# Three column pairs taken together at the FFN's start, another tail, and a crossed placement of every second head pair in PSUM

## The chip, the cores and the metric

The kernel runs on one core of a Trainium2 chip. The metric is the device time of one execution in microseconds (us); the time before is the median of three timed runs. One further execution was recorded by the hardware profiler, and every row that is quoted comes from it. Engines go by short names: PE is TensorE's matrix multiply, PEld its weight load, DVE is VectorE, ACT is ScalarE, POOL is GpSimd, SP is the queue that issues most of the DMAs.

## The reference, cut to what matters

One layer of a hybrid decoder is applied to a prompt of 256 tokens and to 8 x 4 decoded tokens. All 288 tokens go through the same weights.

```python
h = _rmsnorm(x, norm_pre_mix)
z = h @ w_in                                            # 2048 -> 8480 columns
ya, new_wkv = _rwkv7_branch(zs_mix, st_wkv, ...)        # 16 heads of 64, a state [64, 64] each
yb, new_pool = _pool_branch(zp, st_pool, ...)
m = sigmoid(zga) * (ya @ w_branch_a) + sigmoid(zgb) * (yb @ w_branch_b)
x = x + _rmsnorm(m @ w_out, norm_post_mix)
gate, up = split(_rmsnorm(x, norm_pre_ffn) @ w_ffn_in)  # 2048 -> 2 x 5632
f = (gelu(conv(gate)) * up) @ w_ffn_out
x = x + _rmsnorm(f, norm_post_ffn)

def step(s, inp):                                       # the scan of the RWKV-7 branch, per token
    r_t, w_t, k_t, v_t, a_t, b_t = inp
    sa = einsum('bhvk,bhk->bhv', s, a_t)
    s = s * w_t[:, :, None, :] + sa[..., None] * b_t[:, :, None, :] + v_t[..., None] * k_t[:, :, None, :]
    return s, einsum('bhvk,bhk->bhv', s, r_t)
```

## The kernel before, in words

**Dense work.** Channels lie on the 128 partitions, the 288 tokens (`N`) on the free axis. A weight column block of 128 outputs is a list of *units*, each 4 k-tiles of 128x128. A unit is loaded by SP (`load_to`, L176, `raw`), split into two fp32r parts `whi` (ACT, L199) and `wlo` (DVE, L200) by `split_to`, and used by `three` (L259): `whi`·`xh`, `whi`·`xl`, `wlo`·`xh`, three matmuls of 288 columns per k-tile. `take(u)` (L264) splits three units ahead and loads nine ahead. `dense` makes one output column in one PSUM bank; `dense_together` (L288) makes several columns side by side, unit by unit, so that each x part that arrives late is used for all columns.

**PSUM.** There are eight banks: pool `psa` has three (tag `acc`), `psb` three (tag `s`), `psg` two (tag `g`).

**RWKV.** The 16 heads are worked on in four groups `g` of four heads: `i` in 0, 1 is the channel tile (a pair of heads), `par` in 0, 1 the head of the pair, which lies on partitions 0-63 or 64-127 (`HALF`). For each group `front` prepares decay, keys and receptances (`AR`, `KB`), `late` forms the products `ps_g` (L637), a triangular inverse on DVE (L699 to L702; a trip through DRAM, `dA` and `dW`), then the four-chunk `chain` (`ps_x`, `ps_u`, `ps_s`, `ps_y`) and, beside it, `sample` for the decoded tokens (`ps_sg`, `ps_sl`, `ps_st`), and `finish` normalizes and transposes the outputs (`ps_yt`). These generators are stepped by three lanes from inside the dense work: `lane2`, with `late`, makes two steps for each unit, and `yield n` waits n steps. So these small matmuls stand between dense ones in PE's queue. The lanes fix the order in which the program is written down; a scheduler then orders each engine's queue by its own estimate, and an instruction under `pin` stays behind what was written before it on its engine. All queues run in order.

**Where small matmuls sit.** A matmul with 64 rows of weights and 64 outputs uses one quarter of the array: its input half gives the rows, the PSUM half that it writes gives the columns. Before, head `par` reads half `par` and writes half `par` (`ps_sg`, `ps_st`, `ps_y`, `ps_yt`) for both `i`, or reads one half and writes all 128 outputs (`ps_g`).

**The turn.** After the 16 columns of `w_out` (L1165), `rstd_of` (L348) sums the squares over partitions with a matrix of ones, takes a root on ACT and a reciprocal on DVE; `second_parts(k)` (L1185) makes the residual `x2[k]` and its parts `xh`, `xl`; `second_squares` sums their squares for the next norm. `dense_together` then takes the first four `w_ffn_in` columns (two pairs of gate and up).

**The tail** (L1286 to L1311): `rstd_spread` (L359) makes the last scale with tiny matmuls and spreads it into PSUM; DVE multiplies it into the four quarters `fq`, and the residual is added on PE (with the identity), on POOL or on DVE before SP stores the tile.

Of the kernel before, what the change touches and what calls it, by code (L numbers as in the profile page):

```python
# [18 lines left out]
P = 128  # L19
# [22 lines left out]
FA = 2  # L42
BT = 5
IWAIT = 3
IWORK = 300
# [61 lines left out]
def hybrid_step(ctx: ExitStack, tc: tile.TileContext, t):  # L107
# [56 lines left out]
    for f0, nf in THIRDS:  # L164
        ins = []
        if f0 == 0:
            u = add_together([wf[0], wf[NF], wf[1], wf[NF + 1]])
            ins = [(u[0], u[1]), (u[2], u[3])]
# [5 lines left out]
    cursor = {"load": 0, "split": 0}  # L174

# [13 lines left out]
    def split_to(u):  # L189
        while cursor["split"] <= min(u, len(units) - 1):  # L190
# [5 lines left out]
            hi = wp.tile([P, UK, P], F32R, tag="whi", name="whi", bufs=4)  # L196
            lo = wp.tile([P, UK, P], F32R, tag="wlo", name="wlo", bufs=4)
# [66 lines left out]
    def take(u):  # L264
        split_to(u + 3)
        load_to(u + 9)
# [65 lines left out]
    last = [None]  # L332

    def scaled_parts(k, src, scale, where=xp):
        h, l = (where.tile([P, N], F32R, tag=f"x{p}{k}", name=f"x{p}{k}") for p in "hl")
        act.activation(out=h, in_=src, func=AF.Copy, scale=scale)
# [166 lines left out]
    heads = [(i, par) for i in range(G) for par in range(2)]  # L503
    ready, past, k2 = {}, set(), []

    def front(g, rr, kx, vv, lora):
# [21 lines left out]
        ps = psb.tile([P, NC2 + G, 2], F32, tag="s", name="ps_n")  # L528
        for i, par in heads:
            h, o = HALF[par], HALF[1 - par]  # L530
            for c in range(NCH):
                pe.matmul(ps[o, c * G + i], sq[h, i, c * C:(c + 1) * C], ones[h, 0:2], start=True, stop=True)
        for i, par in heads:
            h = HALF[par]
            pe.matmul(ps[UR[par], NC2 + i], sq[h, i, TP:], ones[h, 0:2], start=True, stop=True,
                      tile_position=(h.start, UR[par].start))
# [4 lines left out]
        for par in range(2):  # L541
            dve.tensor_scalar(wr[UR[par], NC2:], ps[UR[par], NC2:, 0:1], 1e-24, None, op0=ALU.max)
            dve.reciprocal(wr[UR[par], NC2:], wr[UR[par], NC2:])
# [78 lines left out]
    def late(g):  # L622
        yield lambda: g in ready
        yield 4
# [6 lines left out]
        for c2 in range(0, NCH, 2):  # L631
            pss = [psg.tile([P, 2 * G, 2 * C], F32, tag="g", name="ps_g") for _ in range(2)]
            for dc in range(2):
                c = c2 + dc
                for i, par in heads:
                    h = HALF[par]
                    pin(pe.matmul(  # L637
                        pss[par][:, dc * G + i, :],
                        KB[h, c, i, :, :].rearrange("p s t -> p (s t)"),
                        AR[h, :, i, c * C:(c + 1) * C],  # L640
                        start=True, stop=True,
                    ))
# [35 lines left out]
        psv = psb.tile([P, G, C], F32, tag="s", name="ps_sv")  # L678
        for i, par in heads:
            h = HALF[par]  # L680
            pe.matmul(psv[VR[par], i], vv[h, i, TP:], ident[h, h], start=True, stop=True, tile_position=(h.start, VR[par].start))
        for par in range(2):
            act.copy(out=UV0[VR[par]], in_=psv[VR[par]])
# [6 lines left out]
        def inverse():  # L690
# [6 lines left out]
            for tt in range(1, 32):  # L697
# [6 lines left out]
                if work > IWORK:  # L704
                    work = 0
                    yield
# [26 lines left out]
        def sample():  # L733
# [14 lines left out]
            ps = psb.tile([P, 3, G, C], F32, tag="s", name="ps_sg")  # L748
            for i, par in heads:
                h = HALF[par]  # L750
                pin(pe.matmul(ps[h, 0, i], KBs[h, i].rearrange("p s t -> p (s t)"), AR[h, :, i, TP:], start=True, stop=True))
            for i, par in heads:
                h = HALF[par]
                pin(pe.matmul(ps[h, 1, i], KBd[h, i].rearrange("p s t -> p (s t)"), ident[h, h], start=True, stop=True))
            for i in range(G):
                for b in range(NB):
                    for par in range(2):
# [673 lines left out]
```

## Time and profile before

| | us |
|---|---|
| median of three timed runs | 1668.98 (1668.06 to 1670.8) |
| the profiled execution, its own time | 1666.09 |
| its span, first to last instruction | 1664.3 |
| PE busy | 1627.8 |
| DVE busy | 1104.5 |
| ACT busy | 814.6 |
| POOL busy | 382.0 |

PE's busy time counts from the start of a matmul to its end, and neighbours overlap: a dense matmul is shown as 0.30 us long, but the next one starts 0.13 us after it. So the distance from start to start is what tells what a piece of PE's work costs. A row of the timeline gives start, duration, engine, line, operation, tiles and count, and in brackets the idle time of the engine before it with the instruction that ended it. An fp32 matmul (not fp32r) is two records. PEclk is the clock that TensorE was granted, 1.00 at full speed.

### The profile page before, as it was taken

How to read it: one execution, taken by the hardware profiler on the slowest of the kernel's cores; microseconds unless marked ns; L12 is line 12 of the kernel's file. 1: busy time of each engine (PE TensorE's matmuls, PEld its weight loads, DVE VectorE, ACT ScalarE, POOL GpSimd, SP SyncE). 2: the span in 40 equal slices, each digit the busy share in tenths (PEclk: the TensorE clock that was granted, in tenths of full speed). 3: DMA queues.
4: the chain of work that ended last, by engine and by line, in shares of the span. 5: the costliest groups of instructions: out<-in, count | busy, mean ns of one | idle time of the engine just before them, and what ended most of it. 6: DMA issues, size and time to landing. Idle time of an engine off the chain costs nothing.

```text
span 1664.3 us, 35679 instructions
## 1 busy us (share of the span) xinstructions
PE 1627.8 (98%) x13398; PEld 1589.1 (95%) x13398; DVE 1104.5 (66%) x2192; ACT 814.6 (49%) x1492; POOL 382.0 (23%) x629
## 2 busy tenths in 40 slices
PE   7999999999999999999899999999999999999998
PEld 6989989989989999999799999999999999999997
DVE  6799778778777857644876665446666555666654
ACT  5544445445445435545565554445545433455554
POOL 4593452343242022400321110001111000111112
PEclk9999999999999999999899999999999999999999
DMA  7435445435535548744254445554444555444553
GB/s 245 159 114 185 157 160 178 158 122 187 188 109 184 189 145 275 236 165 165 96 178 166 166 165 168 167 166 165 167 168 166 166 166 168 165 167 165 176 167 105
DMA packets 157229, 278.95 MB, mean 168 GB/s; under 512 B 25584, under 2 KB 32240, under 8 KB 157056
## 3 DMA queue, kind: packets, MB, share of 16 engines
q1 hardware_dynamic: 151104, 259.16, 48.6%
q0 software_dynamic: 5664, 16.77, 2.8%
q8 instruction: 105, 1.72, 0.4%
q10 hardware_dynamic: 288, 0.74, 0.1%
q14 instruction: 68, 0.56, 0.1%
HBM read 262.67 MB, written 13.93 MB: 166 GB/s over the span
## 4 chain that ended last, share of the span: by engine, by line
PE 88%; DVE 5%; POOL 2%; DMA 2%; issue 1%; ACT 0%; SPq 0%; DVEq 0%; POOLq 0%
PE acc L262 27%; PE acc L260 27%; PE acc L261 27%; DVE wlo L200 1%; DVE wt L699 1%; DMA dW<-wt 1%; PE ps_g L637 1%; DVE wt L702 0%; PE ps_sg L759 0%; POOL win L998 0%; PE ps_s L877 0%; DMA W<-dW 0%; PE ps_st L807 0%; PE ps_y L892 0%; PE ps_u L867 0%
## 5 line engine op out<-in xcount | busy, mean ns | idle before, releaser
L200 DVE TENSOR_TENSOR wlo<-raw,whi 128x512 fp32r<-128x512 f32 x928 | 655.3, 709 | 416.3 <-ACT whi L199 407.6
L199 ACT CAST whi<-raw 128x512 fp32r<-128x512 f32 x928 | 572.7, 619 | 696.5 <-PE acc L261 650.3
L260 PE MATMUL acc<-xh,whi 128*128 128x288 f32 x2736 | 814.8, 299 | 14.1 <-ACT whi L199 9.0
L262 PE MATMUL acc<-xh,wlo 128*128 128x288 f32 x2736 | 812.1, 297 | 5.2 <-DVE wlo L200 5.2
L261 PE MATMUL acc<-xl,whi 128*128 128x288 f32 x2736 | 812.3, 297 | 0.0
L260 PEld LDWEIGHTS acc<-xh,whi 128*128 128x128 f32 x2736 | 517.3, 189 | 18.7 <-ACT whi L199 9.6
L262 PEld LDWEIGHTS acc<-xh,wlo 128*128 128x128 f32 x2736 | 520.2, 190 | 9.9 <-DVE wlo L200 6.1
L261 PEld LDWEIGHTS acc<-xl,whi 128*128 128x128 f32 x2736 | 521.3, 191 | 1.5 <-issue 0.3
L262 PE MATMUL acc<-ah,wlo 128*128 128x288 f32 x704 | 208.7, 296 | 0.0
L260 PE MATMUL acc<-ah,whi 128*128 128x288 f32 x704 | 208.0, 296 | 0.0
L261 PE MATMUL acc<-al,whi 128*128 128x288 f32 x704 | 205.2, 292 | 0.0
L1223 POOL COPY cout<-gt 128x2 f32<-128x2 f32 x44 | 30.8, 700 | 591.7 <-DVE gt L1219 591.7
L261 PEld LDWEIGHTS acc<-al,whi 128*128 128x128 f32 x704 | 134.2, 191 | 0.0
L260 PEld LDWEIGHTS acc<-ah,whi 128*128 128x128 f32 x704 | 132.2, 188 | 0.0
L262 PEld LDWEIGHTS acc<-ah,wlo 128*128 128x128 f32 x704 | 131.9, 187 | 0.0
L1231 POOL TENSOR_TENSOR cv<-cv,rstd_ffn 128x288 f32<-128x288 f32 x44 | 36.8, 837 | 73.9 <-ACT cv L1230 73.1
L699 DVE TENSOR_TENSOR wt<-wt,Ab 128x16 f32<-128x16 f32 (+30 forms) x124 | 52.6, 425 | 1.3
L442 POOL TENSOR_TENSOR df<-zt 128x256 f32<-128x256 f32 (+1 forms) x27 | 23.1, 855 | 100.3 <-DVE zt L440 80.0
L1227 DVE SCALAR_TENSOR_TENSOR cv<-gt,vec,cv 128x255 f32<-128x255 f32 x88 | 43.0, 489 | 0.0
L1188 POOL TENSOR_TENSOR x<-x,og 128x288 f32<-128x288 f32 x11 | 12.9, 1171 | 114.8 <-DVE og L1187 114.8
L262 PE MATMUL acc<-ybh,wlo 128*128 128x288 f32 x128 | 38.2, 298 | 0.7 <-DVE wlo L200 0.7
L260 PE MATMUL acc<-ybh,whi 128*128 128x288 f32 x128 | 38.8, 303 | 0.0
(309 smaller groups left out, 1589.1 us busy)
## 6 DMA issues: line engine op xcount, KB each, us to landing
raw<-in_w_ffn_in SPq DMA_DIRECT2D x352, 256.0 KB, 3.0
raw<-in_w_in SPq DMA_DIRECT2D x264, 256.0 KB, 3.4
raw<-in_w_ffn_out SPq DMA_DIRECT2D x176, 256.0 KB, 2.7
raw<-in_w_out SPq DMA_DIRECT2D x64, 256.0 KB, 3.0
raw<-in_w_branch_b SPq DMA_DIRECT2D x32, 256.0 KB, 3.0
raw<-in_w_branch_a SPq DMA_DIRECT2D x32, 256.0 KB, 4.0
xr<-in_xT SPq DMA_DIRECT2D x8, 288.0 KB, 5.6
tga<-th POOLq DMA_DIRECT2D x16, 144.0 KB, 3.6
```

Of the source, the lines that this page charges most:

```text
L199: act.copy(out=hi[:, a:b, :m], in_=w[:, a:b, :m])
L200: dve.tensor_tensor(lo[:, a:b, :m], w[:, a:b, :m], hi[:, a:b, :m].bitcast(F32), op=ALU.subtract)
L260: pe.matmul(ps, hi, xh, start=start, stop=False)
L261: pe.matmul(ps, hi, xl, start=False, stop=False)
L262: pe.matmul(ps, lo, xh, start=False, stop=stop)
L442: pool.tensor_tensor(df[:m, :TP], zt[:m, 0:TP], zt[:m, 1:ZB], op=ALU.subtract)
L637: pin(pe.matmul(pss[par][:, dc * G + i, :], KB[h, c, i, :, :].rearrange("p s t -> p (s t)"), AR[h, :, i, c * C:(c + 1) * C], start=True, s ...
L699: dve.tensor_tensor(tmp[:, :, :n], Wb[:, :, :n], Ab[:, :n, tt].unsqueeze(1).to_broadcast([P, 8, n]), op=ALU.mult)
L1188: (dve if k < 2 or k % 4 == 0 else pool).tensor_tensor(x2[k], x2[k], og[k], op=ALU.add)
L1223: pool.tensor_copy(cout[:, f, 0:2], gt[:, TP - 2:TP])
L1227: dve.scalar_tensor_tensor(cv[:, s:TP], gt[:, 0:TP - s], w, cv[:, s:TP], op0=ALU.mult, op1=ALU.add)
L1231: pool.tensor_tensor(cv, cv, rst3, op=ALU.mult)
```

## The change

It has these parts.

1. At the turn three pairs, six columns (`TOG`), are made together in place of four. `dense_by_k` goes k-tile by k-tile through all six columns in the first unit, two k-tiles at a time after it. For that, `look` makes `take` split six units ahead from column 14 of `w_out` on, and odd units take their parts from a further SBUF pool `wp2`.
2. `rst2` comes from `rstd_spread`; `second_parts` is queued so that `x2[0]` comes directly after the first product; the squares for the next norm are queued behind all parts.
3. The tail multiplies all four quarters first; then nine tiles get their residual on PE, three on DVE, four on POOL; stores are of one or two tiles.
4. `side(i, par)` puts the second pair (`i` = 1) on the other PSUM half: `ps_n` (decoded part), `ps_sv`, `ps_sg`, `ps_st`, `ps_y`, `ps_yt`. The two pairs then write two banks, one from `psb` and one from `psg`, or two from `psg`. `ps_g` is cut into 64x64 pieces in the order (half 0, half 0), (1, 1), (0, 1), (1, 0). `ps_w` and `ps_n` move from `psb` to `psg`. In `ps_y` the product with `UV` comes ahead of the one with the state.
5. Pace: the inverse yields by `IWORK` 370 with its remainder kept (300 before, remainder dropped); `late(0)` starts after 9 steps, not 4, and waits 11, not 16, ahead of the transposes; two more groups of matmuls (`ps_w12`, `ps_x` with `UV`) are pinned.

```diff
+TOG = 3
-IWORK = 300
+IWORK = 370
...
+            where = late_pool[0] if late_pool and i % 2 else wp
+            hi = where.tile([P, UK, P], F32R, tag="whi", name="whi", bufs=4)
...
     def take(u):
-        split_to(u + 3)
-        load_to(u + 9)
+        split_to(u + look[0])
+        load_to(u + look[0] + 6)
...
+    def dense_by_k(uss, xh, xl, pools):
+        pss = [p.tile([P, 512], F32, tag=tag, name="acc") for p, tag in pools]
+        for c in range(len(uss[0])):
+            w = []
+            step = 2 if c else 1
+            for j0 in range(0, 4, step):
+                for i, (ps, us) in enumerate(zip(pss, uss)):
+                    if j0 == 0:
+                        w.append(take(us[c]))
+                    for j in range(j0, j0 + step):
+                        k = 4 * c + j
+                        three(ps[:, :N], w[i][0][:, j], w[i][1][:, j], xh[k], xl[k], k == 0, k == KD - 1)
+                    if j0 + step == 4:
+                        advance()
+        return pss
...
+    def side(i, par):
+        return par ^ (i % 2)
...
-                ps = psb.tile([P, 512], F32, tag="s", name="ps_w")
+                ps = psg.tile([P, 512], F32, tag="g", name="ps_w")
...
-        yield 4
+        yield 4 if g else 9
...
-                for i, par in heads:
-                    h = HALF[par]
-                    pin(pe.matmul(
-                        pss[par][:, dc * G + i, :],
-                        KB[h, c, i, :, :].rearrange("p s t -> p (s t)"),
-                        AR[h, :, i, c * C:(c + 1) * C],
-                        start=True, stop=True,
-                    ))
+                for i in range(G):
+                    for par, slot in ((0, 0), (1, 1), (0, 1), (1, 0)):
+                        h = HALF[par]
+                        pin(pe.matmul(
+                            pss[par][HALF[slot], dc * G + i, :], KB[h, c, i, slot, :], AR[h, :, i, c * C:(c + 1) * C],
+                            start=True, stop=True,
+                        ))
...
-                if work > IWORK:
-                    work = 0
-                    yield
+                if work >= IWORK:
+                    yield work // IWORK
+                    work %= IWORK
...
-            ps = psb.tile([P, 3, G, C], F32, tag="s", name="ps_sg")
+            pst = [psg.tile([P, 3, C], F32, tag="g", name="ps_sg") for _ in range(G)]
...
+            for b in range(NB):
+                for i, par in heads:
+                    h, q = HALF[par], HALF[side(i, par)]
+                    pin(pe.matmul(pst[i][q, 2], arm[h, i, b * C:(b + 1) * C], S0[h, i, b, :], start=b == 0, stop=b == NB - 1))
...
+            for i, par in heads:
+                h, q = HALF[par], HALF[side(i, par)]
+                pin(pe.matmul(psts[i][h], BKs[q, i], uxs[i][q], start=True, stop=True))
...
-        yield 2 * WWAIT + (0 if g else 16)
+        yield 2 * WWAIT + (0 if g else 11)
...
+                psy = [p.tile([P, 512], F32, tag=tag, name="ps_y") for p, tag in ((psb, "s"), (psg, "g"))]
+                for i, par in heads:
+                    pe.matmul(
+                        psy[i][HALF[side(i, par)], 0:C], Gm[:, par, c * G + i, 0:C], UV[:, c * G + i, par, :],
+                        start=True, stop=c == 0,
+                    )
                 if c:
                     for i, par in heads:
                         h = HALF[par]
+                        pe.matmul(
+                            psy[i][HALF[side(i, par)], 0:C], AR[h, 0, i, c * C:(c + 1) * C], S[h, i, :],
+                            start=False, stop=True,
+                        )
...
                 for par in range(2):
-                    h, r = HALF[par], slice(64 * par, 64 * par + 32)
-                    pe.matmul(ps[h, TP:N], Yt[r, NC2 + i, :], ident[r, r], start=True, stop=True, tile_position=(h.start, h.start))
+                    h, q = HALF[par], HALF[side(i, par)]
+                    pe.matmul(ps[h, TP:N], Yt[q, NC2 + i, :], ident[q, q.start:q.start + 32], start=True, stop=True)
...
+        if j == 14:
+            look[0] = 2 * TOG
+            late_pool.append(wp2)
...
-    rst2 = rstd_of([acc2, sq], "post", ep)
+    rst2 = rstd_spread([acc2, sq], ep)
...
-        with tc.issue_after(paced[k - AHEAD]) if k >= AHEAD else ExitStack():
+        with tc.issue_after(paced[k - AHEAD] if k >= AHEAD else ends[0]) if k else ExitStack():
             dve.tensor_tensor(og[k], og[k], rst2, op=ALU.mult)
...
+        with tc.issue_after(last[0].ins), tc.issue_after(last_hi[0].ins):
+            for k in range(KD):
+                second_squares(k)
...
-                    pss = dense_together(uss, xh, xl, [(psa, "acc")] * 2 + [(psg, "g")] * 2)
+                    pss = dense_by_k(uss, xh, xl, [(psa, "acc")] * 3 + [(psg, "g")] * 2 + [(psb, "s")])
...
+    on_pe = {0: psg, 1: psg, 2: psa, 4: psa, 5: psa, 8: psb, 9: psg, 14: psg, 15: psa}
+    on_dve = (11, 12, 13)
...
     for q in range(4):
         pin(dve.tensor_tensor(fq[q], fq[q], rst4.unsqueeze(1).to_broadcast([P, 4, N]), op=ALU.mult))
+    for j in range(16):
+        if j in on_pe:
...
+            pin(pe.matmul(sums[j][:, :N], ident, f_sb[j], start=False, stop=True))
+            pin(act.copy(out=f_sb[j], in_=sums[j][:, :N]))
+        else:
+            pin((dve if j in on_dve else pool).tensor_tensor(f_sb[j], f_sb[j], x2[j], op=ALU.add))
...
+        if j in (1, 5, 9, 15):
+            store(j - 1, 2)
+        elif j not in (0, 4, 8, 14):
+            store(j)
```

More of the change, by code (lines that the diff above doesn't have):

```diff
@@ L174, in hybrid_step @@
     cursor = {"load": 0, "split": 0}
+    late_pool, look = [], [3]
     def load_to(u):
@@ L526, in front @@
                 act.activation(out=dst[:, i], in_=ps[:, :N], func=AF.Tanh, scale=0.5, bias=der[:, row, m:m + 1])
-        ps = psb.tile([P, NC2 + G, 2], F32, tag="s", name="ps_n")
+        ps = psg.tile([P, NC2 + 1, 2], F32, tag="g", name="ps_n")
         for i, par in heads:
@@ L532, in front @@
                 pe.matmul(ps[o, c * G + i], sq[h, i, c * C:(c + 1) * C], ones[h, 0:2], start=True, stop=True)
+        psn = [psg.tile([P, 2], F32, tag="g", name="ps_ns"), ps[:, NC2]]
         for i, par in heads:
             h = HALF[par]
-            pe.matmul(ps[UR[par], NC2 + i], sq[h, i, TP:], ones[h, 0:2], start=True, stop=True,
-                      tile_position=(h.start, UR[par].start))
+            pe.matmul(psn[i][HALF[side(i, par)]], sq[h, i, TP - 32:], ones[h, 0:2], start=True, stop=True)
         wr = kp.tile([P, NC2 + G, 1], F32, tag="wr", name="wr", bufs=2)
@@ L677, in late @@
             act.copy(out=UV[HALF[par], :, par, :], in_=ps[HALF[par]].rearrange("p (a v) -> p a v", v=C))
-        psv = psb.tile([P, G, C], F32, tag="s", name="ps_sv")
+        psv = [p.tile([P, C], F32, tag=tag, name="ps_sv") for p, tag in ((psb, "s"), (psg, "g"))]
         for i, par in heads:
[L680 to L683, printed above, removed]
+            h, r = HALF[par], VR[side(i, par)]
+            pe.matmul(psv[i][r], vv[h, i, TP:], ident[h, h], start=True, stop=True, tile_position=(h.start, r.start))
+        for i in range(G):
+            for r in VR:
+                act.copy(out=UV0[r, i], in_=psv[i][r])
         yield 3
@@ L772, in sample @@
             for i in range(G):
-                act.activation(out=BKs[:, i], in_=ps[:, 1, i], func=AF.Copy, scale=wr[:, NC2 + i])
+                act.activation(out=BKs[:, i], in_=pst[i][:, 1], func=AF.Copy, scale=wr[:, NC2 + i])
             for i in range(G):
@@ L803, in sample @@
             for i in range(G):
-                pst = psb.tile([P, NB, C], F32, tag="s", name="ps_st")
-                for par in range(2):
-                    h = HALF[par]
-                    pin(pe.matmul(pst[h], BKs[h, i], uxs[i][h], start=True, stop=True))
-                psts.append(pst)
+                psts.append(psb.tile([P, NB, C], F32, tag="s", name="ps_st"))
+            for i, par in heads:
+                h, q = HALF[par], HALF[side(i, par)]
+                pin(pe.matmul(psts[i][h], BKs[q, i], uxs[i][q], start=True, stop=True))
             for i in range(G):
@@ L1284, in hybrid_step @@
     pool.dma_start(out=t["o_conv"], in_=cout)
-    banks = [(psg, "g"), (psg, "g"), (psa, "acc"), (psa, "acc"), (psb, "s"), (psa, "acc"), (psg, "g"), (psg, "g")]
+    on_pe = {0: psg, 1: psg, 2: psa, 4: psa, 5: psa, 8: psb, 9: psg, 14: psg, 15: psa}
+    on_dve = (11, 12, 13)
+    tags = {id(psg): "g", id(psa): "acc", id(psb): "s"}
     sums = {}
```

91 lines of the change are left out of this document (38 added, 53 removed).

## The prediction, on record before the changed kernel was run

> **What bounds the kernel now.** I read the page's first part, then a table of busy times by stretch, the list of PE's waits, and the timeline where PE waits.
>
> ```profile
> PE 1627.8 (98%) x13398; PEld 1589.1 (95%) x13398; DVE 1104.5 (66%) x2192; ACT 814.6 (49%) x1492; POOL 382.0 (23%) x629
> ...
> 700.00:1640.00 940.00, 932.78 (x7000) 930.75 (x6999) 560.02 (x1034) 471.63 (x828) 98.87 (x158) 0.99 0.51 163
> ```
>
> PE is the bound over the whole run. In the second row, the first number after the stretch is its length, then PE's busy time and its records, at the end the granted clock: 7000 dense matmuls in 940 us, 0.134 us each, and but for the turn at its start there is nothing to win there. The change touches none of these matmuls. It can win where PE waits, where its clock is halved, and in the small matmuls between the dense ones.
>
> ```profile
> PE ps_g L637 <- DVE AR L581: 5.4, 2, 3.3
> ...
> PE ps_q L826 <- DVE tq L820: 2.7, 4, 1.7
> ...
> 101.50:108.30 6.80, 6.19 (x29) 5.39 (x30) 6.80 (x11) 0.00 (x0) 6.70 (x12) 0.50 0.38 108
> ...
> 449.66:453.07 3.41, 3.41 (x16) 3.41 (x16) 1.36 (x3) 1.80 (x5) 1.07 (x2) 0.50 0.76 234
> 484.90:487.24 2.34, 0.22 (x15) 0.12 (x6) 2.31 (x4) 0.00 (x0) 2.34 (x3) 0.99 0.00 0
> 487.24:490.65 3.41, 3.41 (x22) 3.19 (x22) 3.41 (x6) 0.60 (x2) 1.93 (x3) 0.50 0.12 43
> 801.23:808.06 6.83, 6.03 (x25) 6.03 (x26) 6.83 (x14) 5.00 (x12) 2.89 (x4) 0.50 0.00 0
> 814.88:818.30 3.42, 3.31 (x14) 3.31 (x15) 3.42 (x8) 1.81 (x4) 1.02 (x2) 0.50 0.41 138
> ```
>
> The waits are small (total us, times, longest), but each gap is followed by 3.4 or 6.8 us at clock 0.50, in which a dense matmul takes twice as long.
>
> **The change part by part, the turn.** These are its rows, in order of time, and two rows of the tail, which uses `rstd_spread` already.
>
> ```profile
> 794.61 0.69 DVE L200 TENSOR_TENSOR wlo<-raw,whi 128x512 fp32r<-128x512 f32 x1 [0.91 <-ACT whi L199]
> ...
> 796.08 0.40 ACT L1159 ACTIVATE sq<-acc 128x288 f32<-128x288 f32 x1
> ...
> 797.86 1.95 DVE L354 RECIPROCAL rstd_post<-rstd_post 128x288 f32<-128x288 f32 x1 [0.96 <-ACT rstd_post L353]
> 799.85 1.20 DVE L1187 TENSOR_TENSOR og<-og,rstd_post 128x288 f32<-128x288 f32 x3
> 800.96 1.41 DVE L1188 TENSOR_TENSOR x<-x,og 128x288 f32<-128x288 f32 x2
> 802.30 0.51 DVE L337 SCALAR_TENSOR_TENSOR xl<-x,vec,xh 128x288 fp32r<-128x288 f32 x1
> ...
> 831.25 0.51 DVE L337 SCALAR_TENSOR_TENSOR xl<-x,vec,xh 128x288 fp32r<-128x288 f32 x1
> ...
> 802.03 1.33 PE L260 MATMUL acc<-xh,whi 128*128 128x288 f32 x4 [4.74 <-ACT xh L336]
> ...
> 812.49 0.40 PE L260 MATMUL acc<-xh,whi 128*128 128x288 f32 x1 [1.14 <-ACT whi L199]
> ...
> 814.99 0.61 PE L262 MATMUL acc<-xh,wlo 128*128 128x288 f32 x1 [0.93 <-DVE wlo L200]
> ...
> 1648.81 0.44 ACT L1159 ACTIVATE sq<-f 128x288 f32<-128x288 f32 x1 [3.74 <-DVE f L1274]
> ...
> 1652.00 2.62 DVE L1299 TENSOR_TENSOR f<-f,ps_spread 128x1152 f32<-128x1152 f32 x2 [0.84 <-PE ps_spread L376]
> ```
>
> *Start.* From the end of the last square (796.48) to the first product with the scale (799.85) it is 3.37 us, 1.95 of them the reciprocal over 288 columns. `rstd_spread` takes 1649.25 to 1652.00, 2.75 us: 0.62 less. Then DVE makes three products ahead of `x2[0]`, 1.11 us; with `x2[0]` behind one of them it is 0.37: 0.74 less. The gap ends 1.36 us sooner, at 800.67.
>
> *Supply.* The first and the last of the 16 `xl` lie 28.95 us apart, 1.93 us per k-tile, with the squares and the weight splits among them. Four columns use up a k-tile in 12 x 0.134 = 1.61 us, so PE outruns it: the two idle times, 1.14 and 0.93. Six columns take 18 x 0.134 = 2.41 us. PE no longer catches up, even if the squares cost DVE what they cost now, and they go behind. I take 2.07 us. The three units split ahead cost DVE 3 x 0.69 us where it idles 0.91 of every 1.6; without that idle time they would add 2 us. The pass is over near 842, the last square some ten us before, so the next scale is in time. All three `psa` banks are then taken, but column 0 is complete 30 matmuls (4.0 us) ahead of column 5, and its reader takes under 1 us; if the scale came late, PE would lose that 1 us.
>
> *Clock.* From 802.03 to 808.06 and from 814.88 to 818.30 PE ran at half: 3.0 + 1.7 us lost. The second goes with the waits. One stays, between 3.4 and 6.8 us long: 1.7 to 3.4, I take 2.6. Gain 2.1. Idle time of 2.34 us (484.90 to 487.24) was enough for a halved clock here. The Trainium skill, "TensorE: Matmul & The Clock Gate", Part 1, has the clock halved after an idle window of about 3.4 us that runs freely; by it the new gap of some 3.5 us may cover no whole window, and the row with 2.34 us speaks against reading it so strictly.
>
> Turn: 1.36 + 2.07 + 2.1 = **5.5 us**, between 3 and 8.
>
> **The tail.**
>
> ```profile
> 1656.00:1658.00 2.00, 1.39 (x6) 1.12 (x7) 1.97 (x3) 0.74 (x2) 1.07 (x1) 1.00 0.99 356
> 1658.00:1660.00 2.00, 2.00 (x10) 1.45 (x8) 0.78 (x2) 0.80 (x2) 1.07 (x1) 1.00 0.98 350
> ...
> 1660.74 0.33 SPq L1306 DMA_DIRECT2D o_y<-f  x1
> ```
>
> The last product comes sooner, since DVE does four in a row: 1652.00 + 4 x 1.31 = 1657.2. But the last two columns say that the DMA engines are 98% busy with the output at 350 GB/s from 1656 on, so earlier results wait there. Nothing at least; at most the 1.1 us of two adds that stood between the products (DVE was 1.97 us busy in the first of these stretches). I take **0.5 us**.
>
> **The small matmuls.** Each pair of rows gives a cost as the distance of two starts.
>
> ```profile
> 325.56 0.69 PE L838 MATMUL ps_w<-W,tq 32*32 32x32 f32 x30
> 326.18 0.27 PE L857 MATMUL ps_x<-UV,Gm 64*64 64x64 f32 x2
> ...
> 326.71 2.03 PE L759 MATMUL ps_sg<-S,arm 64*64 64x64 f32 x64
> 328.58 0.40 PE L867 MATMUL ps_u<-X,W 64*64 64x64 f32 x8
> ...
> 342.47 0.45 PE L890 MATMUL ps_y<-S,AR 64*64 64x64 f32 x8
> 342.85 0.45 PE L892 MATMUL ps_y<-UV,Gm 128*64 128x64 f32 x8
> 343.23 0.45 PE L786 MATMUL ps_sl<-UVs,Gs 64*64 64x64 f32 x8
> ...
> 363.19 1.45 PE L807 MATMUL ps_st<-ux,BKs 64*64 64x512 f32 x6
> 364.57 0.40 PE L262 MATMUL acc<-xh,wlo 128*128 128x288 f32 x1
> ...
> 368.15 1.16 PE L637 MATMUL ps_g<-AR,KB 64*128 64x128 f32 x16
> 369.24 0.40 PE L262 MATMUL acc<-xh,wlo 128*128 128x288 f32 x1
> ```
>
> - Changes of form. 64 records of one form take 1.87 us, 29 ns each. Eight should take 0.23; between blocks of other forms (64*64, 128*64) they take 0.38, so a change costs 0.15. With the `UV` product first it stands beside `ps_s`, which has its form, and the state product beside `ps_sl`: two changes less in chunks 1 to 3 of four groups, 12 x 0.30 = 3.6; I take 3.0, since the scheduler may put other work between. The decoded part of `ps_yt` gets its neighbours' form: one change, eight times, 0.9 with the shorter block left out. `ps_x` pinned out of `ps_w12`: 0.2 x 4 = 0.8.
> - Four quarters. Now two heads run side by side. `ps_st`: three steps in 1.38 us, 0.46 each, four per group; with all quarters at once two. That is up to 0.9 x 4 = 3.7, nothing at least; I take 2.4, two thirds, as one step in four seems hidden beside `ps_x`. `ps_sg`: between 29 ns and the 21 ns of the 30 records of `ps_w12`: up to 0.5 x 4 plus the 16 records beside it, 2.7; nothing at least; half, 1.4. `ps_g`: 16 records in 1.09 become 32 half as wide; at 29 ns 0.93, a gain of 0.16 in each of eight blocks, 1.2; if only two ran at a time, 32 x 68 ns = 2.2, a loss of 8.7; I take +0.6.
> - No row shows two quarters that share an array half at work together. The Trainium skill, "TensorEngine Tiling (Array Packing)", Key Properties, lets different tiles work in parallel; by it `ps_st` would come to its upper bound.
>
> Together **9.1 us**. The added ACT copies (one per chunk, three per group, some 0.3 us each) lie beside an ACT that is 49% busy; on a full ACT they would be some 8 us. The two added steps a group on DVE (`wr`) are of a few elements.
>
> **Pace and waits.** Waits of 5.4 and 2.7 us and 13.6 us at half clock (6.8 lost) make 14.9 us. How much goes is open: these matmuls stand where the scheduler's estimate puts them, and DVE ends them.
>
> ```profile
> 102.79 2.07 PE L637 MATMUL ps_g<-AR,KB 64*128 64x128 f32 x14 [0.27 <-POOL KB L595]
> 104.79 0.61 PE L261 MATMUL acc<-dl,whi 128*128 128x288 f32 x1
> ...
> 107.21 1.27 DVE L644 TENSOR_TENSOR Gm<-ps_g,con 128x512 f32<-128x512 f32 x2
> ...
> 398.00:441.00 43.00, 43.00 (x327) 43.00 (x326) 42.13 (x113) 19.11 (x33) 14.43 (x33) 1.00 0.53 171
> ```
> *First `ps_g`.* Five more lane steps put it some 4 us later (two steps for a unit of 12 matmuls, 1.6 us). But DVE is busy for all of 101.50 to 108.30, and the next dense matmul in the queue, with `dl` from DVE, could start at 104.79 only: when `ps_g` stands elsewhere, that wait is late next. *`ps_q` and the fourth group's `ps_g`.* In the inverse DVE is busy for 42.13 of 43.00 us, so a slower pace in the program does not make it end sooner; it helps only where it moves `ps_q` in the queue. I take a fifth, **3.0 us**, between -2 (a wait at a worse place) and 14.9. Seven more steps in each of four inverses (12152 units of work by 370 make 32 or 33 steps, before 26) end the last group up to 28 steps, 23 us, later; `w_branch_a` needs it. Cover are its first halves of five columns, 60 matmuls or 8 us, and what distance the last group has from it now; with the 8 us alone it would cost up to 15 us. I take nothing, since the lanes hand out the steps and DVE, not they, ends a group.
>
> *A wait that is added.* `psg` has two banks. Before, it served only `ps_g` in these groups; now also `ps_w`, `ps_n`, `ps_sv`, `ps_sg` and half of `ps_y`: 13 takes a group, 52 in all. Behind a take that waits, the whole of PE's queue stands, dense matmuls too. In the rows above `ps_g` ends at 104.86 and DVE frees its two banks at 107.21 + 1.27 = 108.48, 3.6 us later. There are eight such pairs: nothing to 29 us; nearest to nothing, since no two takes are written close to each other but by the pace of the lanes, **-1.5 us**.
>
> Sum: 5.5 + 0.5 + 9.1 + 3.0 - 1.5 = 16.6 us. The profiled execution took 1666.09 us, 1.79 more than its span, and 2.89 less than the median of 1668.98. So 1666.09 - 16.6 = 1649.5 for such an execution, and 1649.5 + 2.9 = **1652.4** for a median.
>
> **The rivals.**
>
> - *The waits go too.* Speaks for it: each halved clock follows a gap, so removing a short wait saves its shadow as well. Against: DVE's full stages. Another 11.9 us: 1640.5.
> - *Only two quarters run at a time.* For: every row shows pairs. Against: 21 ns a record in `ps_w12` is less than the 29 of 64*64, so PE can take records faster. Loses 8.7 + 0.6 at `ps_g`, 2.4 at `ps_st`, 1.4 at `ps_sg`: 1652.4 + 13.1 = 1665.5.
> - *The scheduler undoes it.* The change does not do what it says if the scheduler puts other forms between the blocks again, or draws the squares ahead of the parts at the turn: gains of 5 of the 9.1 and of 3 of the 5.5 us go, 1660.
> - *The `psg` banks become the wait (slower).* Place: a `ps_y`, `ps_w` or `ps_sg` behind `ps_g` in PE's queue; price 3.6 us per `ps_g` pair. For: the scheduler can place a `ps_g` early, amid the chain of the group before, and that chain now needs the same banks. Against: none of PE's waits before was for a bank. All eight: 28.8 - 1.5 more, 1680. It decides from the sixth pair on (1.5 + 16.6 = 18.1 us, 5.03 pairs).
> - *The clock is not halved at the turn*, by the skill's rule above read strictly: 2.6 less, 1649.8, inside the forecast's own range.
>
> **How the numbers follow.** Forecast, 1646 to 1658: 0.58, with the rival of the clock, 0.05, in it besides. The waits go too: 0.12. Scheduler: 0.09. Two quarters: 0.08, half of it within 0.2% of before. Banks: 0.08. 0.2%, 3.3 us, is about what a measurement of this kernel can tell from no change. Faster: 0.58 + 0.05 + 0.12 + 0.09 + 0.04 = 0.88; same 0.04; slower 0.08. The range from 1641 to 1666 leaves out the banks, 0.08, and the lower part of the first rival, some 0.08.
>
> **What would show it.** Right: at the turn, the bracket of the first `acc<-xh` near 3.4 us and no PE wait for `whi` or `wlo` in the pass after it, one halved clock there; the `xl` rows done well ahead of PE; `ps_y` with `UV` directly behind `ps_s`, no change of form between; `ps_st` in half its 1.4 us; the output DMA still near 350 GB/s. Wrong: 32 records of `ps_g` in over 1.1 us (two quarters only); idle PE ahead of a `psg` tile ended by `Gm`, `UV0` or `Yt`; a wait of `yah` matmuls for the last group; the first `ps_g` wait in place again, as `dl`.

## The result, and the profile after

The changed kernel took **1657.23 us** (median of 4 runs, 1653.36 to 1658.32), beside 1668.53 for the kernel before on the same chip: a ratio of 0.9924, interval 0.9906 to 0.9943. The forecast was 1652.4 in a range from 1641 to 1666. So 11.3 us of the forecast 16.6 came. Six more runs of the changed kernel gave a median of 1655.78, ratio 0.9925 (0.9908 to 0.9942).

The profiled execution after took 1656.41 us and has a span of 1654.6, 9.7 less than before. First its busy times, then the list of what TensorE (PE) waited for: total us, times, longest.

```profile
PE 1614.3 (98%) x13540; PEld 1578.4 (95%) x13540; DVE 1103.4 (67%) x2201; ACT 816.2 (49%) x1521; POOL 372.7 (23%) x628
```

```profile
PE acc L263 <- DVE zb L1021: 8.5, 2, 7.8
PE acc L263 <- ACT whi L202: 8.2, 1, 8.2
PE acc L265 <- DVE wlo L203: 6.5, 6, 3.3
PE ps_q L852 <- DVE tq L846: 3.1, 3, 2.5
PE ps_g L665 <- DVE AR L608: 2.6, 1, 2.6
PE acc L263 <- ACT xh L356: 1.6, 1, 1.6
...
PE ps_sv L707 <- DVE Gm L670: 0.7, 1, 0.7
PE ps_g L665 <- ACT Yt L928: 0.5, 1, 0.5
...
PE ps_g L665 <- DVE Gm L670: 0.4, 1, 0.4
```

PE is 13.5 us less busy (1627.8 before), and the span only 9.7 shorter: some of what was saved has become idle time. The first row is new: 8.5 us in which two dense matmuls waited for `zb` on VectorE (DVE), one of them 7.8 us. The wait of the first `ps_g` for `AR`, 3.3 us at the longest before, has gone from that place, and a longer one stands beside it. Only the last three rows name a bank of `psg` that another engine had yet to read, 1.6 us together.

The stretches at half clock, from the table of busy times by stretch (us, then PE, PE's weight loads, DVE, ACT, POOL with their records, then the clock):

```profile
88.77:92.18 3.41, 3.41 (x16) 3.41 (x16) 3.27 (x11) 0.33 (x1) 2.11 (x5) 0.50 0.01 2
102.43:112.67 10.24, 5.12 (x21) 5.15 (x22) 9.64 (x14) 1.63 (x3) 9.99 (x17) 0.50 0.32 89
225.30:228.71 3.41, 3.41 (x30) 3.16 (x30) 3.08 (x9) 0.21 (x1) 3.18 (x4) 0.50 0.41 128
447.17:454.00 6.83, 6.83 (x55) 6.49 (x54) 2.86 (x6) 3.74 (x8) 1.07 (x2) 0.50 0.81 231
795.40:802.20 6.80, 5.33 (x22) 5.33 (x23) 6.73 (x15) 3.22 (x6) 3.14 (x4) 0.50 0.00 2
```

They make 30.7 us within the span, as much as before. At the turn one is left of two; in the RWKV stage there is more, 10.24 us around the new wait alone.

**The turn and the tail.** PE's timeline at the turn, the row of the 16 `xl` (ns least, median, most; first and last start), and two stretches of the end:

```profile
791.61 0.30 PE L265 MATMUL acc<-xh,wlo 128*128 128x288 f32 x1
791.75 0.59 PE L384 MATMUL ps_sum<-con,acc 128*96 128x2 f32 x6
792.79 0.67 PE L384 MATMUL ps_sum<-con,sq 128*96 128x2 f32 x6 [0.45 <-ACT sq L1191]
794.51 0.75 PE L396 MATMUL ps_spread<-dg,con 96*128 96x288 f32 x2 [1.04 <-DVE dg L392]
796.87 1.81 PE L263 MATMUL acc<-xh,whi 128*128 128x288 f32 x6 [1.61 <-ACT xh L356]
```

```profile
L357 DVE SCALAR_TENSOR_TENSOR xl<-x,vec,xh x16: 506/692/1061, 797.4 to 817.2; 128x288 fp32r<-128x288 f32 x16
```

```profile
1646.00:1648.00 2.00, 2.00 (x10) 1.56 (x9) 2.00 (x2) 1.26 (x4) 2.00 (x3) 1.00 0.67 247
1648.00:1650.00 2.00, 2.00 (x10) 1.55 (x9) 1.37 (x4) 0.86 (x3) 0.12 (x1) 1.00 1.04 358
```

From the last matmul of `w_out` to the first of the feed-forward it was 6.67 us (795.36 to 802.03); now it is 796.87 - 791.61 = 5.26, 1.41 less. From this first matmul of the feed-forward to the 288th behind it (as many as the six columns have) it took 46.27 us and takes 42.45. DVE makes an `xl` every 1.32 us (19.8 over 15), and PE needs one in 2.41: only two idle times for weights are left in the pass, 0.23 and 0.28 us. At the end the output moves at 358 GB/s, as it did (350 to 356).

**The small matmuls.** Their rows in PE's timeline:

```profile
324.85 0.98 PE L785 MATMUL ps_sg<-S,arm 64*64 64x64 f32 x54
325.66 0.22 PE L893 MATMUL ps_u<-X,W 64*64 64x64 f32 x1
...
357.16 0.65 PE L834 MATMUL ps_st<-ux,BKs 64*64 64x512 f32 x2
...
357.39 1.02 PE L834 MATMUL ps_st<-ux,BKs 64*64 64x512 f32 x5
358.34 0.40 PE L263 MATMUL acc<-xh,whi 128*128 128x288 f32 x1
```

```profile
339.04 0.45 PE L903 MATMUL ps_s<-UV,BK 128*64 128x64 f32 x8
339.32 0.40 PE L914 MATMUL ps_y<-UV,Gm 128*64 128x64 f32 x8
339.65 0.34 PE L921 MATMUL ps_y<-S,AR 64*64 64x64 f32 x8
339.82 0.40 PE L813 MATMUL ps_sl<-UVs,Gs 64*64 64x64 f32 x8
```

54 records of `ps_sg` start within 0.81 us (324.85 to 325.66), 15 ns each, where it was 29: four quarters do run together. `ps_st` takes 1.18 us, 1.38 before. In the second block each product of `ps_y` stands beside a neighbour of its own form, and the two take 0.50 us (339.32 to 339.82) where they took 0.76.

To see where time goes I add up, for each PE record, the distance from its start to the next start, as far as the 4500th dense matmul (in `w_out`, behind the whole RWKV stage). Distances behind a small matmul give "small"; of those behind a dense one, what is over 0.1325 us gives "excess", which holds waits and half clock:

| us, to the 4500th dense matmul | small | of it `ps_sg` | `ps_st` | `ps_yt` | excess |
|---|---|---|---|---|---|
| before | 109.2 | 9.29 | 5.69 | 6.76 | 42.2 |
| after | 95.3 | 5.30 | 4.19 | 4.17 | 52.2 |

The small matmuls lost 13.9 us, more than forecast, and the excess grew by 10.0. It grew by idle time: PE's gaps of more than 0.15 us behind dense matmuls make 13.0 us before and 23.1 after, while half clock cost the dense ones 7.6 and costs 8.2. With the waits and the half clock taken out of the first column too, the small matmuls' own work fell from 104.5 to 93.3 us, by 11.2. What made the idle time is what the experiments ask about.

### The profile page after: what moved, and what is told of

It is laid out like the page before. It is cut to its first block, busy times and chain, and to the rows that moved or that the text cites. A ratio compares the mean times of both kernels' runs of the same rounds, so it can differ in the third digit from the quotient of the medians.

```text
span 1654.6 us, 36001 instructions
## 1 busy us (share of the span) xinstructions
PE 1614.3 (98%) x13540; PEld 1578.4 (95%) x13540; DVE 1103.4 (67%) x2201; ACT 816.2 (49%) x1521; POOL 372.7 (23%) x628
## 4 chain that ended last, share of the span: by engine, by line
PE 73%; DVE 2%; issue 1%; DMA 0%; ACT 0%; POOL 0%; DVEq 0%; POOLq 0%; SPq 0%; ACTq 0%
PE acc L265 23%; PE acc L263 23%; PE acc L264 23%; DVE wlo L203 1%; DVE xl L357 0%; DVE og L1223 0%; PE ps_y L1347 0%; DMA dW<-wt 0%; PE ps_y L1333 0%; DVE wt L726 0%; PE ps_s L903 0%; PE ps_g L665 0%; DVE wt L729 0%; PE ps_v L701 0%; PE ps_x L883 0%
## 5 line engine op out<-in xcount | busy, mean ns | idle before, releaser
L263 PEld LDWEIGHTS acc<-xh,whi 128*128 128x128 f32 x2736 | 517.1, 189 | 23.7 <-issue 10.6
L264 PE MATMUL acc<-ybl,whi 128*128 128x288 f32 x128 | 38.3, 300 | 0.0
```

The source lines that it names most:

```text
L263: pe.matmul(ps, hi, xh, start=start, stop=False)
L264: pe.matmul(ps, hi, xl, start=False, stop=False)
```

## The experiments

Times are medians of 4 to 12 runs, ratios are to the kernel before on the same chip (its median was 1668.2 to 1668.5 in all of them). Theories: the **DVE theory** (DVE sets the pace of the stage, and what PE saves it waits a little later), the **pace theory** (the new pace costs), and the **bank theory** (the new takes of the two `psg` banks cost).

**The turn and the tail alone.** The kernel before with `rstd_spread`, `dense_by_k`, the look-ahead pool and the new tail; RWKV is untouched.

> The kernel of before with only the turn, its look-ahead pool and the tail changed; RWKV as before. From the two traces at equal dense counts the turn gave 5.3 us and the tail 0.8: 1668.5 - 6.1 = 1662.4, range 1661.5 to 1663.5. Were the turn's gain larger than that and the RWKV stage's change a loss, it would be 1657 or less; were the turn's gain only lent by a better start from the RWKV stage, 1665 or more.

1662.35 us, ratio 0.9965 (0.9949 to 0.9982). That is 6.2 us less than before, where the forecast had 5.5 + 0.5. These parts are settled and add up. So the RWKV stage's change is worth 1662.35 - 1657.23 = 5.1 us (6.6 with the second set of runs), where the forecast had 9.1 + 3.0 - 1.5 = 10.6. Its profiled execution, 1658.13, is the shortest of its 8 runs; so I take times from medians and only places from traces.

**The pace of before.**

```diff
-IWORK = 370
+IWORK = 300
-    yield 4 if g else 9
+    yield 4
-                if work >= IWORK:
-                    yield work // IWORK
-                    work %= IWORK
+                if work > IWORK:
+                    work = 0
+                    yield
-        yield 2 * WWAIT + (0 if g else 11)
+        yield 2 * WWAIT + (0 if g else 16)
```

> The changed kernel with the pace of before: the inverse's quantum 300 with the remainder dropped, 4 steps ahead of the first ps_g in group 0 and 16 ahead of its inverse's end. DVE theory (what TensorE saves in the small matmuls, it waits for DVE a little later, wherever the small matmuls stand): the time stays within 1.5 us of the changed kernel's 1657.2, and the first ps_g waits for AR again in place of the dense matmul that waits for the mix. Pace theory (the new pace itself took the missing 7 us): 1650 to 1654, 3 to 7 us faster than the changed kernel. The third possibility, that the new pace gave the 3.0 us that I had put down to it: 1659 to 1661.

1658.25 us, ratio 0.9937 (0.992 to 0.9955): 1.0 slower than the first set of the changed kernel, 2.5 than the second. The pace theory falls; the time lies within the DVE theory's band. PE's timeline in the first group (start, us, and in brackets the wait and what ended it):

```profile
83.62 0.41 PE L263 MATMUL ps_w<-zwa_h,lo_h 64*128 64x288 f32 x2
...
87.31 0.40 PE L263 MATMUL ps_w<-zwa_h,lo_h 64*128 64x288 f32 x1
...
108.71 1.99 PE L665 MATMUL ps_g<-AR,KB 64*64 64x128 f32 x32 [7.30 <-DVE AR L608]
```

The 7.8 us for `zb` have become 7.3 for `AR`, behind the same DVE queue. The new pace moved this wait and hardly made it longer or shorter. (The rows of `ps_w` are needed further down.)

**No pair crossed.** `side` returns `par`. So that two quarters that share columns do not write one bank, the tiles of `ps_ns` stand in `psb`, which the expectation does not mention.

```diff
-        return par ^ (i % 2)
+        return par
-        psn = [psg.tile([P, 2], F32, tag="g", name="ps_ns"), ps[:, NC2]]
+        psn = [psb.tile([P, 2], F32, tag="s", name="ps_ns") for _ in range(G)]
```

> The changed kernel with no pair crossed: each head of the second pair keeps its own half, so two quarters run at a time where four did (sample, states, ps_y, ps_yt; the first scores keep their four quarters by key and token). TensorE's own time in these rows grows by about 3.7 (ps_sg) + 1.5 (ps_st) + 1.1 (ps_y from S) + 2.6 (ps_yt, both kinds) = 8.9 us less what the new forms alone gave, some 6 us. DVE theory: most of it is hidden in waits that shrink, 1657.2 + 1 to 3 = 1658 to 1660. If TensorE bounds the stage: + 5 to 9, 1662 to 1666.

1655.85 us, ratio 0.9922 (0.9904 to 0.994): not slower at all, though in the trace `ps_sg` is back at 9.35 us, `ps_st` at 5.69, and all small matmuls at 103.1. The excess is 44.8 instead of 52.2: 7.8 us more behind small matmuls, 7.4 us less excess. The time lies below the bands of both theories. It is nearer to the DVE theory, but two edits are mixed here; below they are taken apart.

**The lora products and norms in three banks.** `ps_w`, `ps_n` and `ps_ns` are taken from `psb` again.

```diff
-                ps = psg.tile([P, 512], F32, tag="g", name="ps_w")
+                ps = psb.tile([P, 512], F32, tag="s", name="ps_w")
-        ps = psg.tile([P, NC2 + 1, 2], F32, tag="g", name="ps_n")
+        ps = psb.tile([P, NC2 + 1, 2], F32, tag="s", name="ps_n")
-        psn = [psg.tile([P, 2], F32, tag="g", name="ps_ns"), ps[:, NC2]]
+        psn = [psb.tile([P, 2], F32, tag="s", name="ps_ns"), ps[:, NC2]]
```

> The changed kernel with the lora products ps_w and the norms ps_n, ps_ns in the pool with three banks again, as before the change. Bank theory (takes of the two banks cost the missing 7 us): 1654 or less. DVE theory: within 1 us of 1657.2, for the waits that name these banks add up to under 2 us in the trace.

1651.37 us, ratio 0.9897 (0.9881 to 0.9913). This is 4.4 to 5.9 us less than the changed kernel, the shortest median of all the kernels here. Its interval and that of the changed kernel overlap slightly, but the runs lie apart: 1649.96 to 1652.36, and 1653.36 to 1658.32. With it the RWKV stage's change is worth 1662.35 - 1651.37 = 11.0 us. The DVE theory, which put it within 1 us, had no room for this. Yet PE still waits for DVE in the first group; the largest wait there is now

```profile
PE acc L264 <- DVE dl L366: 6.1, 1, 6.1
```

In the traces the waits up to the 4500th dense matmul make 24.1 us, as against 23.8 in the changed kernel. What is less is the half clock between 70 and 700 us: 10.2 us long where it was 23.9.

**The changed kernel again, and the norms alone.** The second moves `ps_n` and `ps_ns` to `psb`, and leaves `ps_w` in `psg`.

```diff
-        ps = psg.tile([P, NC2 + 1, 2], F32, tag="g", name="ps_n")
+        ps = psb.tile([P, NC2 + 1, 2], F32, tag="s", name="ps_n")
-        psn = [psg.tile([P, 2], F32, tag="g", name="ps_ns"), ps[:, NC2]]
+        psn = [psb.tile([P, 2], F32, tag="s", name="ps_ns"), ps[:, NC2]]
```

> The changed kernel itself once more, beside the runs it is compared with: 1657.2 within 1 us. Were it at 1653 or less, the 5.9 us by which the kernel with ps_w and ps_n in the pool of three banks beat it would be mostly a difference between chips, and the bank theory would lose its evidence.

> The changed kernel with only the norms ps_n and ps_ns in the pool of three banks again; the lora products ps_w stay in the two banks of psg. Bank theory, if the take of the norms is the costly one (three psg takes behind one another at the end of front, of which each holds a bank until DVE has read it): 1651 to 1653. If the lora products are the costly ones: 1656 to 1658.

1655.78 (ratio 0.9925, given above), 0.4 below the band that I had put around 1657.2; and 1653.2, ratio 0.9906 (0.9888 to 0.9924). The chips agree, so the gain of 4.4 to 5.9 us is none of theirs. The norms give 2.6 to 4.0 of it, just outside the band of 1651 to 1653, and the lora products some 1.8; the intervals overlap in both steps, so the split is rough.

**VectorE relieved.** In both kernels rows 8 to 31 of the inverse are left out, 2 x 24 DVE instructions in each of four groups; the pace keeps its steps.

```diff
+                if tt < 8:
                     dve.tensor_tensor(
                         tmp[:, :, :n], Wb[:, :, :n], Ab[:, :n, tt].unsqueeze(1).to_broadcast([P, 8, n]), op=ALU.mult
                     )
                     dve.tensor_reduce(out=Wb[:, :, tt], in_=tmp[:, :, :n], op=ALU.add, axis=AX.X)
```

> The kernel with the turn and tail alone (RWKV as before), and of the inverse only rows 1 to 7 computed: rows 8 to 31 are left out, some 170 instructions' worth of 31 to 36 us of VectorE in each of four groups, with the steps of the pace as they were. DVE theory and bank theory both: VectorE is no longer full during the inverse, and the time falls from 1662.4 by what TensorE waited for it there, 3 to 12 us: 1650 to 1659. This run counts by its difference to the next.

> The changed kernel with the same rows 8 to 31 of the inverse left out. The RWKV stage's change is worth 1662.4 - 1657.2 = 5.1 us with the whole inverse. DVE theory (the rest of the 14 us that TensorE saves in small matmuls goes into waits for VectorE): with VectorE relieved on both sides the difference to the run before grows to 9 to 14 us. Bank theory: the two banks are as short as ever, the difference stays at 4 to 7 us.

1654.57 (0.9919, 0.9901 to 0.9937) and 1651.9 (0.9901, 0.9883 to 0.9919): a difference of 2.7, below what either theory gave (the intervals of the two overlap). The two groups of DVE rows that make the inverse (busy us, mean ns, idle us before them), in the kernel with the turn and the tail alone, and in the same with the rows left out:

```profile
L719 DVE TENSOR_TENSOR wt<-wt,Ab 128x16 f32<-128x16 f32 (+30 forms) x124 | 52.4, 422 | 1.3
L722 DVE TENSOR_REDUCE wt<-wt 128x8 f32<-128x16 f32 (+30 forms) x124 | 36.0, 291 | 1.6
```

```profile
L720 DVE TENSOR_TENSOR wt<-wt,Ab 128x16 f32<-128x16 f32 (+6 forms) x28 | 7.1, 255 | 0.5
L723 DVE TENSOR_REDUCE wt<-wt 128x8 f32<-128x16 f32 (+6 forms) x28 | 5.4, 194 | 0.5
```

DVE was relieved of 75.9 us, 19 in each group (not the 31 to 36 that I had expected). The times fell by 7.8 and by 3.9 to 5.3 us, so a full DVE in the inverse does cost some. But it is not what kept the small matmuls' gain back, or the difference would have grown. In the changed kernel so relieved, the largest wait still is

```profile
PE acc L263 <- DVE zb L1022: 9.2, 2, 8.5
```

and it lies at 100 us, before the first inverse has begun. DVE's work there was not relieved, so these two runs answer the DVE theory for the inverse and leave it untested for the end of `front`.

**Crossing once more, with the banks given back.** As the kernel with three banks, and `side` returns `par`; each `ps_ns` has a tile of `psb` of its own.

```diff
-        return par ^ (i % 2)
+        return par
-        psn = [psb.tile([P, 2], F32, tag="s", name="ps_ns"), ps[:, NC2]]
+        psn = [psb.tile([P, 2], F32, tag="s", name="ps_ns") for _ in range(G)]
```

> The kernel with ps_w, ps_n and ps_ns in the pool of three banks (1651.4), and no pair crossed. The earlier run without crossing came to 1655.9, as fast as the changed kernel, but its ps_ns stood in the three banks too, so two edits were mixed. Bank theory (crossing pays, and the takes had hidden it): 1654.5 to 1658, 3 to 6 us slower than 1651.4. Were crossing worth nothing in time, though it saves some 8 us of TensorE: 1650.5 to 1653.

1659.63 us, ratio 0.9948 (0.993 to 0.9967): without crossing, 8.3 slower. With only the norms in `psb` the nearest pair is 1655.85 against 1653.2, 2.7; there `ps_n` stands in `psg` without crossing and in `psb` with it, and the intervals overlap. So crossing does pay, 2.7 to 8.3 us; the upper end holds one more take of `psb` at the end of `front`, for the second `ps_ns`. It also means that `psb` is not better for `ps_w` and `ps_n` in itself: without crossing they are 3.8 us faster in `psg`.

**The pace of before, with the banks given back.** The kernel with three banks, with the edit to the pace shown above.

> The kernel with ps_w, ps_n and ps_ns in the pool of three banks (1651.4), with the pace of before. Forecast's step (the pace gives 3.0 us once nothing else is in the way): 1653.5 to 1655.5. DVE theory for the pace (a wait moved is a wait kept): 1650.5 to 1652.5. In the changed kernel the old pace cost 1.0 to 2.5 us.

1651.98 us, ratio 0.9902 (0.9885 to 0.992), 0.6 from 1651.37. The new pace is worth 0 to 2.5 us, not 3.0.

**Five takes alone.** The kernel with the turn and the tail, in which only `ps_w` and `ps_n` are taken from `psg`.

```diff
-                ps = psb.tile([P, 512], F32, tag="s", name="ps_w")
+                ps = psg.tile([P, 512], F32, tag="g", name="ps_w")
-        ps = psb.tile([P, NC2 + G, 2], F32, tag="s", name="ps_n")
+        ps = psg.tile([P, NC2 + G, 2], F32, tag="g", name="ps_n")
```

> The kernel with the turn and tail alone (1662.4), and of the RWKV change only the pool of the lora products ps_w and the norms ps_n: five takes a group from the two banks of psg in place of the three of psb. No matmul changes. Bank theory: this alone costs 3 to 6 us, 1665 to 1668. If the takes hurt only beside the other takes that the change adds: 1662 to 1664.

1660.52 us, ratio 0.9954 (0.9939 to 0.9969): no loss, rather 1.8 less than 1662.35, though the intervals overlap. A take of `psg` has no fixed price; the bank theory in that form falls too. Yet the traces show how the banks work in the first group. PE's timeline there, with `ps_w` and `ps_n` in `psb` (turn and tail alone), and then in `psg`:

```profile
83.57 0.41 PE L263 MATMUL ps_w<-zwa_h,lo_h 64*128 64x288 f32 x2
...
84.08 0.29 PE L263 MATMUL ps_w<-zwa_h,lo_h 64*128 64x288 f32 x1
...
102.89 0.76 PE L657 MATMUL ps_g<-AR,KB 64*128 64x128 f32 x2 [3.32 <-DVE AR L601]
```

```profile
82.53 0.41 PE L263 MATMUL ps_w<-zwa_h,lo_h 64*128 64x288 f32 x2
...
86.23 0.40 PE L263 MATMUL ps_w<-zwa_h,lo_h 64*128 64x288 f32 x1
...
107.06 2.08 PE L657 MATMUL ps_g<-AR,KB 64*128 64x128 f32 x16 [6.67 <-DVE AR L601]
```

With three banks the last of these `ps_w` stands 0.5 us behind the first, with two 3.7 us: a third tile has to wait until ACT has read one, and the scheduler puts dense matmuls between (in the second trace ACT had read one at 83.74, and the product stands at 86.23). So no wait for a bank shows in the list. But all that hangs on `ps_w` comes later, down to `AR`: the first `ps_g` starts 19.3 us behind the first `ps_w` with three banks and 24.5 with two, and PE stands for 6.67 us instead of 3.32. The rows of the changed kernel with the pace of before, further up, have the second form: 3.7 us, 25.1, and 7.30 of waiting. With the banks given back, and the same pace, it is the first form again:

```profile
81.05 0.41 PE L263 MATMUL ps_w<-zwa_h,lo_h 64*128 64x288 f32 x2
...
81.55 0.29 PE L263 MATMUL ps_w<-zwa_h,lo_h 64*128 64x288 f32 x1
...
100.20 0.44 PE L665 MATMUL ps_g<-AR,KB 64*64 64x128 f32 x6 [2.83 <-DVE AR L608]
103.48 0.61 PE L264 MATMUL acc<-dl,whi 128*128 128x288 f32 x1 [2.84 <-DVE dl L366]
```

19.2 us and a wait of 2.83, with a second one of 2.84 for `dl` right behind: 5.7 us in place of 7.3. In this pair only the pool of `ps_w` and the norms differs; it makes the front of the first group 5.9 us longer. At the new pace `AR` is done 25.0 us behind the first of these `ps_w` in the changed kernel, 21.5 with the norms alone in `psb`, and 19.1 with `ps_w` there too.

What this costs can be read at equal counts. From the 450th to the 1000th dense matmul, which holds this stretch and ends ahead of the first chain, the five traces with `ps_w` and all the norms in `psg` took 95.8 to 97.4 us (the changed kernel 96.7 and 96.6). The six with `ps_ns` or more of them in `psb` took 92.4 to 93.5, and the stage as it was, with its inverse whole, 90.9 and 91.5. The run without crossing is one of the six, with 93.0: moving its `ps_ns` spared it 3.7 us here, and from there to the 4500th it took 580.6 us where the changed kernel took 578.0, 2.6 more. So in these traces the two edits that were mixed in it had opposite effects, and the run looked as if crossing was worth nothing.

**All takes in `psb`.** As the kernel with three banks, but `ps_sv`, `ps_sg` and `ps_y` are in `psb` too.

```diff
-        psv = [p.tile([P, C], F32, tag=tag, name="ps_sv") for p, tag in ((psb, "s"), (psg, "g"))]
+        psv = [psb.tile([P, C], F32, tag="s", name="ps_sv") for _ in range(G)]
-            pst = [psg.tile([P, 3, C], F32, tag="g", name="ps_sg") for _ in range(G)]
+            pst = [psb.tile([P, 3, C], F32, tag="s", name="ps_sg") for _ in range(G)]
-                psy = [p.tile([P, 512], F32, tag=tag, name="ps_y") for p, tag in ((psb, "s"), (psg, "g"))]
+                psy = [psb.tile([P, 512], F32, tag="s", name="ps_y") for _ in range(G)]
```

> The kernel with ps_w, ps_n and ps_ns in the pool of three banks (1651.4), with the other takes that the change put into psg (ps_sv, ps_sg, ps_y) there as well; psg keeps only the first scores. Bank theory, if every take of psg costs: 1647 to 1650. If only the takes in the first part of a group cost, since DVE is late there, and the three banks become short in the chain instead: 1652 to 1656.

1671.68 us, ratio 1.0024 (1.0011 to 1.0036): 20 us slower, and slower than before the change, beyond both theories. PE's timeline in the last group, and the clock around the first of these rows:

```profile
652.87 1.18 PE L969 MATMUL ps_yt<-con,Yt 64*64 64x64 f32 x19 [5.98 <-DVE Yt L959]
667.30 0.61 PE L265 MATMUL acc<-yah,wlo 128*128 128x288 f32 x1 [5.03 <-DVE wlo L203]
```

```profile
648.80:659.00 10.20, 6.08 (x56) 5.70 (x57) 5.00 (x10) 3.19 (x5) 1.25 (x3) 0.50 0.06 19
```

Here the group itself ends late: its last `ps_yt` stands at 652.9, with `ps_sv`, `ps_sg` and `ps_y` as in the change at 635.5. PE stands in the rows above for 5.98 and 5.03 us, and both gaps come with half clock. The edit shows that the pools cost this. That the chain ran short of banks, the mechanism of the forecast's slower rival with the other pool as its place, is argued: no wait in this trace names a bank of `psb`.

## Why the prediction was right, and where it was wrong

- **Turn, 5.5 us.** Right, and for its reasons: the start 1.41 us (forecast 1.36; PE's idle time came in three pieces, 1.61 us the longest, where one of some 3.4 was awaited), supply and clock together 46.27 - 42.45 = 3.8 (forecast 2.07 + 2.1). One halved clock is left there, 6.80 us long. The rival by which the clock would not be halved at the turn is refuted.
- **Tail, 0.5 us.** From the last dense matmul to the end it was 16.35 us and is 15.58: 0.8. Alone, turn and tail gave 6.2, in the sum 6.0.
- **Small matmuls, 9.1 us.** The mechanism was right, the size too small: 13.9 us between the two traces, of which 2.1 is a wait inside `ps_sl` that went; 11.2 without waits and half clock. The terms that were off: `ps_sg` gave 4.0 where I took 1.4, since I took 21 ns a record as the least and then half of that gain, and the records came at 15 ns; `ps_yt` 2.6 where I had 0.9, since I counted only its decoded part, and its 128 larger records pack as well. `ps_st` gave 1.5 of 2.4. `ps_g` gave 2.3 where I had 0.6, but 1.8 of it lies in the two blocks that had run at half clock before; the other six gave 0.5. `ps_t` beside it lost 1.3, of which 0.7 is a wait. The changes of form came out as 2.4 of 3.0 (`ps_y` 0.9, `ps_s` 0.9, `ps_sl` 0.6 without its wait).
- **Pace and waits, +3.0 us: this step failed.** It took a fifth of the 14.9 us of waits and half clock to go, and put at nothing the end of `front` that the takes push back. Instead the excess rose from 42.2 to 52.2, by idle time; half clock cost about as much as before. The step had the right sentence in it, that where `ps_g` stands elsewhere a dense matmul behind the full DVE is late next: that is the new wait of 7.8 us, for `zb` and not for `dl`. It then counted on a gain all the same. The pace alone is worth 0 to 2.5 us.
- **The added wait, -1.5 us.** It was looked for in the wrong place: in PE standing before a bank. Of that the trace has the 1.6 us shown above. Giving three banks back to `ps_w` and the norms brings 4.4 to 5.9 us; what is shown of it is the later `AR` of the first group, and 3.2 us less in the traces between the 450th and the 1000th dense matmul. The forecast of 1652.4 holds for that kernel (1651.4) by luck, with other terms: more from the small matmuls, nothing from the pace.
- **The whole.** The stage brought 5.1 to 6.6 us of the forecast 10.6. That 1657.2 lies within the range is owed to the turn and the tail, which came as forecast. In the stage it is in part luck: the step on the waits had the wrong sign, and small matmuls that gave more than forecast covered a part of what the waits took.
- **The rivals.** The waits go too: refuted, they grew. Two quarters only: refuted by 15 ns a record. The scheduler undoes it: its sum, 1660, was near, but `ps_y` does stand beside its form and the turn is as written; it was not that. Banks: half right, as said.

**What stays open.** Why the same two pools come out the other way without crossing (1655.9 in `psg`, 1659.6 in `psb`); the first group is alike in the two traces, 93.0 and 93.4 us, so the difference lies behind it. Why they make no loss in the stage as it was, though the first group took 4.9 us more there (95.8 against 90.9). The chain from `ps_w` to `AR` is shown in the first group; that the halved clock at 447 us in the changed kernel, which the kernels with `ps_w` and the norms or the norms alone in `psb` do not have there, comes from the takes of the third group in the same way is only argued. With the norms alone in `psb` there is as much half clock in the stage as in the changed kernel, at other places, and the waits are shorter; with `ps_w` there too it is the other way round. The time of this stage depends on the order in which the scheduler interleaves the lanes, and a few us of it cannot be put down to one edit.

## What to carry to other kernels

When work is taken off the bounding engine in a stage whose lanes hang on another engine, count the saving once in busy time and once in waits: here 13.9 us of TensorE were saved and 10.0 us came back, nearly all as idle time. Moving a PSUM tile to a pool with fewer banks need not show as a wait for a bank; look for the next product placed later and for whoever waits at the end of its chain. Change the pools of tiles one at a time, since the same move gained 5 us, nothing or lost 4 here, by what stood beside it.

## What was not expected of the hardware

- Four 64 x 64 quarters with fp32 operands start a record every 15 ns (54 records in 0.81 us, two to a matmul); two of them one every 29 ns. So four take half the time that two take, also where they share an array half. By the rule of the Trainium skill that was weighed ("TensorEngine Tiling (Array Packing)", Key Properties) `ps_st` would have come to its bound of 3.7 us; it gave 1.5, and `ps_sg` came beyond its bound, 4.0 of 2.7.
- At the turn the clock was halved at 795.40, though PE's longest idle time there is 1.61 us, between short products of the norm that keep it from standing still. The Trainium skill ("TensorE: Matmul & The Clock Gate", Part 1) asks for an idle window of about 3.4 us; read as a time without any matmul, the trace disagrees.
- Half clock comes in pieces of 3.41 us: 3.41, 6.83 and 10.24 in the rows above. The 10.24 begin 2.6 us after PE stopped (99.79 to 102.43), and last through the rest of the wait and 5.1 us of work. The wait of 2.5 us before `ps_q` was followed by 6.83, from 447.17.
- Runs of one kernel differ by such pieces. The changed kernel's two profiled executions, at 1656.41 and 1657.27 us, have PE's waits within 0.8 us of each other, and 30.7 and 34.1 us at half clock within their spans.
